# A hard-max attention kernel: four query tiles loaded between the first key halves, first transposes copied in half columns by two engines, a group's key chosen in five steps

## The chip, the cores and the metric

The kernel runs on one core of a Trainium2 chip. The metric is device microseconds for one execution, as the median of several. The profile is a separate reading of one such execution: its span, from the first to the last instruction, is 1.7 to 1.9 us less than the time that is measured for the same execution, so spans are compared with spans and medians with medians.

Engines in the profile: PE is TensorE, DVE is VectorE, ACT is ScalarE, POOL is GpSimd, SP is SyncE.

## The reference

```
q, k, v: (4, 4096, 128) float32, normal random numbers
logits = q @ k.transpose            # per batch, 4096 x 4096
out[b, i] = v[b, argmax(logits[b, i])]
```

It is attention whose softmax is replaced by the single best key. Every output row must be the right row of `v`, so near ties have to be found and settled exactly.

## The kernel before

A query tile is 128 queries, and there are 128 tiles in all, 32 to a batch. The 4096 keys of a batch are taken in 1024 groups of four. TensorE multiplies the queries with sums and differences of the keys of a pair, and the larger of the two logits of a pair is the sum part plus the absolute difference part. Per tile this takes three evictions of 128x1024 on ScalarE (two `A`, one `E`) and one on VectorE (`W`, the *fold*, which takes the maximum of the two pairs). `W` carries a score in the upper half of each word and the group's number in the lower half. `MAX8` then gives the best groups of each query.

```
def dpart(t, x):                                  # differences of pair x: |d|
    ps = pp.tile([P, 1024], FP32, tag="u")
    mm(ps, t, 1 + 2 * x, True)
    nc.scalar.activation(out=A, in_=ps, func=AF.Abs)

def spart(t, x):                                  # sums of pair x, plus A
    ...
    if x == 0:
        nc.scalar.activation(out=E, in_=ps, func=AF.Relu, scale=QSCALE)

def fold(t):                                      # VectorE: max of the two pairs
    nc.vector.scalar_tensor_tensor(out=W_t[t % NW].bitcast(I16)[:, 1::2], in0=ps, scalar=QSCALE, in1=E,
                                   op0=OP.mult, op1=OP.max)
def top(t):
    nc.vector.max(out=TOP[:, t, :], in_=W_t[t % NW].bitcast(FP32))
```

For every tile GpSimd then gathers the best group's three key differences (`kg`, fp16). VectorE multiplies them with the queries (`prod`), folds the products twice (`p`) and sums them (`D`). For 8 tiles at a time (4 near the end) it chooses the best of the four keys, and GpSimd gathers that key's row of `v` (`vr`):

```
near = (d + NEAR) >= mx                           # which of the four are near the best
CNT  = sum(near)                                  # over 1: the row is flagged
lt   = d < mx
sel  = lt * 2**20 + iotab[b]
wi   = min(sel)                                   # number of the best, first one of equals
win  = cand * 4 + wi
for j in range(n):
    nc.gpsimd.indirect_dma_start(out=vr[:, j, :], in_=v_flat, in_offset=IOA(ap=win[:, j:j + 1], axis=0))
```

(shortened to formulas; with the maximum `mx` in front these are seven VectorE instructions.) Flagged rows are computed again exactly, in two segments. The second comes at the very end: GpSimd fetches the record `FR`, the query `FQ`, three key groups `FK` and the value `FV` of each flagged row and writes them to the output.

The start-up is what the change mostly rearranges:

```
for h in range(2):
    load_k(0, h, 0, 16)                           # key halves, fp32 -> fp16, GpSimd's queue
load_q(0, 0, 8)                                   # 8 query tiles behind them
load_q(0, 8, NQT)
... warm-up matmuls, identity ...
for h in range(2):
    put_k(0, h)                                   # kd: key differences for the gathers
...
def trn_half(b, u, h):                            # transposes of key unit u, half h
    ...
    if h == 1:
        nc.scalar.activation(out=kT[...1024 columns...], in_=ps, func=AF.Copy)
...
for u in (1, 3, 0, 2):
    trn_half(0, u, 0)
trn_half(0, 1, 1)
trn_q(0, 0)                                       # 8 query tiles, one copy by ScalarE
trn_half(0, 3, 1)
trn_half(0, 0, 1)
dpart(0, 0)
trn_half(0, 2, 1)
dpart(0, 1)
```

## Time and profile before

| | before |
|---|---|
| median | 471.05 us (4 runs, 470.95 to 471.29) |
| span of the profiled run | 469.4 us |
| first fold starts | 19.82 us |
| last fold starts | 416.07 us |
| first gather of the end's flags (`FR`) | 433.66 us |
| final write of the flagged rows | 458.48 us |

The view by windows gives the busy time of each engine in a stretch. Its columns are the stretch, its length, then busy us of TensorE, its weight loads, VectorE, ScalarE and GpSimd, with the number of instructions in brackets, the granted clock, the DMA share and GB/s. Of the kernel before:

```profile
core 0: us, PE busy (x) PEld busy (x) DVE busy (x) ACT busy (x) POOL busy (x), PEclk, DMA share, GB/s
...
60.00:150.00 90.00, 85.08 (x418) 38.18 (x417) 90.00 (x163) 86.68 (x105) 58.57 (x65) 1.00 0.51 99
150.00:300.00 150.00, 138.02 (x674) 61.51 (x673) 149.21 (x288) 139.67 (x166) 108.10 (x119) 1.00 0.60 116
300.00:400.00 100.00, 89.97 (x389) 37.32 (x388) 100.00 (x207) 91.12 (x99) 70.36 (x72) 1.00 0.31 85
```

VectorE is busy 339.2 of 340 us: it sets the pace of the long middle. ScalarE (317.5 us) and TensorE (313.1 us) are not far behind.

The timeline lists instructions by start, with duration and, in brackets, the engine's idle time just before and what ended it. VectorE's start-up, before:

```profile
4.24 1.29 DVE L100 CAST identh<-ident 128x128 f16<-128x128 f32 x1 [3.11 <-POOL ident masks.py:199]
...
19.82 1.31 DVE L224 SCALAR_TENSOR_TENSOR W<-psn,E 128x1024 int16<-128x1024 f32 x1 [8.42 <-ACT E L211]
```

TensorE's, before. The three lines show when the two key halves and the queries have landed (for the first half the wait stands with TensorE's weight load, 0.61 us until 6.52):

```profile
6.53 0.23 PE L151 MATMUL tk<-identh,natk 128*128 128x128 f16 x1
...
8.98 0.23 PE L151 MATMUL tk<-identh,natk 128*128 128x128 f16 x1 [0.49 <-DMA natk<-in_k_dram]
...
11.28 1.04 PE L178 MATMUL tq<-identh,natq 128*128 128x128 f16 x8 [1.67 <-DMA natq<-in_q_dram]
```

ScalarE's, before: the first distance eviction and the first `E`, with a key copy between the evictions (left out).

```profile
15.08 1.04 ACT L198 ACTIVATE A<-pd 128x1024 f16<-128x1024 f32 x1
...
18.69 1.09 ACT L211 ACTIVATE E<-psn 128x1024 int16<-128x1024 f32 x1
```

So VectorE waits for ScalarE, ScalarE for TensorE, and TensorE for the queries, which come last.

The tail belongs to GpSimd. Its timeline near the end, before:

```profile
393.50 0.94 POOL L246 DMA_INDIRECT kg<-k,cand  x1 [0.66 <-DVE near L283]
...
431.16 0.94 POOL L303 DMA_INDIRECT vr<-in_v_dram,win  x1 [0.30 <-issue]
432.41 0.94 POOL L303 DMA_INDIRECT vr<-in_v_dram,win  x1 [0.30 <-issue]
433.66 1.09 POOL L495 DMA_INDIRECT FR<-rec,rr_e  x1 [0.30 <-DVE row_e L492]
```

From 393.50 us to `FR` at 433.66 GpSimd starts 32 gathers and scatters every 1.25 us without another wait: 40.16 us.

### The profile page before, as it was taken

The numbers are of one execution on the slowest core, as the hardware profiler recorded it, in microseconds if no ns is written. First come the engines' busy times: TensorE is split into PE (matmuls) and PEld (weight loads), VectorE is DVE, ScalarE is ACT, GpSimd is POOL, SyncE is SP. The second block draws the span as 40 slices with busy tenths as digits, with TensorE's granted clock in tenths as the row PEclk, the third lists the DMA queues.
The fourth block names the chain that finished last, engine by engine and source line by source line (L and its number), as shares of the span: only waits on it lengthen the run. The fifth ranks groups of instructions, "written<-read, shape, count | busy, mean of one in ns | idle before, by whom it ended". The sixth has DMA issues, their size and how long they took to land. (4 is left out here: it accounts for less than half of the span.)

```text
span 469.4 us, 6266 instructions
## 1 busy us (share of the span) xinstructions
PE 381.8 (81%) x1840; PEld 169.8 (36%) x1840; DVE 417.2 (89%) x845; ACT 379.7 (81%) x438; POOL 305.8 (65%) x345
## 2 busy tenths in 40 slices
PE   7999999999999889999998889999999889920000
PEld 3544444444444334444443434343333333300000
DVE  4189999999999999999999999999999999998400
ACT  1999999999999899999998889999999879910000
POOL 9124445876667887766677876667777567777740
PEclk9899999999999999999999999999999999975555
DMA  7913489462224969642336864232433132324320
GB/s 135 231 31 81 79 129 124 91 137 69 86 74 99 193 110 161 117 113 59 101 92 146 119 123 94 69 98 64 120 90 110 51 100 57 113 66 122 104 79 5
DMA packets 40776, 47.42 MB, mean 101 GB/s; under 512 B 24200, under 2 KB 32395, under 8 KB 40736
## 3 DMA queue, kind: packets, MB, share of 16 engines
q0 software_dynamic: 18464, 30.97, 33.9%
q1 hardware_dynamic: 22272, 16.00, 13.2%
q8 instruction: 15, 0.25, 0.2%
q14 instruction: 25, 0.20, 0.2%
HBM read 39.59 MB, written 12.19 MB: 110 GB/s over the span
## 5 line engine op out<-in xcount | busy, mean ns | idle before, releaser
L198 ACT ACTIVATE A<-pd 128x1024 f16<-128x1024 f32 x256 | 258.8, 1042 | 17.2 <-PE pd L189 17.0
L246 POOL DMA_INDIRECT kg<-k,cand x128 | 126.2, 986 | 100.5 <-DVE p L265 25.2
L224 DVE SCALAR_TENSOR_TENSOR W<-psn,E 128x1024 int16<-128x1024 f32 x128 | 167.6, 1309 | 13.1 <-ACT E L211 11.9
L189 PE MATMUL pd<-kT,qT 128*128 128x512 f16 x512 | 152.3, 379 | 15.1 <-ACT A L198 14.4
L189 PE MATMUL psn<-kT,qT 128*128 128x512 f16 x512 | 151.8, 378 | 14.0 <-ACT A L198 9.0
L228 DVE MAX8 TOP<-W 128x8 f32<-128x1024 f32 x128 | 157.5, 1231 | 0.0
L189 PEld LDWEIGHTS <-qT 128*128 128x128 f16 x1024 | 98.5, 97 | 162.0 <-issue 74.7
L208 PE MATMUL psn<-A,identh 128*128 128x512 f16 x512 | 152.1, 378 | 0.0
L303 POOL DMA_INDIRECT vr<-in_v_dram,win x128 | 126.5, 988 | 39.0 <-issue 37.2
L211 ACT ACTIVATE E<-psn 128x1024 int16<-128x1024 f32 x128 | 132.3, 1034 | 5.5 <-PE psn L208 5.1
L208 PEld LDWEIGHTS <-identh 128*128 128x128 f16 x512 | 49.6, 97 | 60.8
L261 DVE TENSOR_TENSOR prod<-kg,natq 128x768 f16<-128x768 f16 x64 | 35.7, 559 | 1.1 <-DMA kg<-k,cand 1.1
L265 DVE TENSOR_TENSOR p<-prod 128x384 f16<-128x384 f16 x64 | 22.9, 361 | 0.0
L270 DVE TENSOR_REDUCE D<-p 128x6 f32<-128x192 f16 x64 | 22.2, 349 | 0.0
L167 ACT ACTIVATE kT<-uk 128x256 f16<-128x256 f32 x48 | 20.1, 418 | 0.9 <-PE uk L164 0.9
L268 DVE TENSOR_TENSOR p<-p 128x192 f16<-128x192 f16 x64 | 16.4, 259 | 0.0
L163 PE MATMUL uk<-identh,natk 128*128 128x128 f16 x96 | 15.8, 218 | 0.5 <-ACT A L198 0.5
L63 POOL DMA_DIRECT2D natk<-in_k_dram x26 | 15.6, 603 | 0.9 <-POOLq L778 0.8
L66 POOL DMA_DIRECT2D natq<-in_q_dram x26 | 15.7, 607 | 0.0
L461 PE MATMUL fp_e<-n_e,tri 128*128 128x1 f32 x2 | 0.6, 361 | 16.2 <-DVE n_e L459 16.2
L164 PEld LDWEIGHTS <-natk 128*128 128x128 f16 x96 | 9.3, 97 | 7.6 <-issue 5.1
L163 PEld LDWEIGHTS <-natk 128*128 128x128 f16 x96 | 9.3, 97 | 5.6
(148 smaller groups left out, 146.8 us busy)
## 6 DMA issues: line engine op xcount, KB each, us to landing
out_dram<-vr SPq DMA_DIRECT2D x14, 512.0 KB, 2.9
k<-kd SPq DMA_DIRECT2D x8, 384.0 KB, 2.6
natk<-in_k_dram POOLq DMA_DIRECT2D x24, 128.0 KB, 3.7
natq<-in_q_dram POOLq DMA_DIRECT2D x24, 128.0 KB, 3.1
kg<-k,cand POOLq DMA_INDIRECT x128, 2.7
vr<-in_v_dram,win POOLq DMA_INDIRECT x128, 3.3
natk<-in_k_dram POOLq DMA_DIRECT2D x2, 512.0 KB, 7.0
out_dram<-vr SPq DMA_DIRECT2D x4, 256.0 KB, 2.1
```

The costliest lines, as they stand in the source:

```text
L163: nc.tensor.matmul(out=o, lhsT=natk[b % 2][:, h, 4 * m + x, :], rhs=identh, start=True, stop=False)
L189: nc.tensor.matmul(out=ps[:, n * 512:(n + 1) * 512], lhsT=qT[b % 2][:, qt * P:(qt + 1) * P], rhs=kT[b % 2][:, u * 1024 + n * 512:u * 1024 ...
L198: nc.scalar.activation(out=A, in_=ps, func=AF.Abs)
L208: nc.tensor.matmul(out=ps[:, n * 512:(n + 1) * 512], lhsT=identh, rhs=A[:, n * 512:(n + 1) * 512], start=False, stop=True)
L211: nc.scalar.activation(out=E, in_=ps, func=AF.Relu, scale=QSCALE)
L224: nc.vector.scalar_tensor_tensor(out=W_t[t % NW].bitcast(I16)[:, 1::2], in0=ps, scalar=QSCALE, in1=E, op0=OP.mult, op1=OP.max)
L228: nc.vector.max(out=TOP[:, t, :], in_=W_t[t % NW].bitcast(FP32))
L246: near_q.append(lambda j=j: nc.gpsimd.indirect_dma_start(out=kg[:, j].rearrange("p f d -> p (f d)"), out_offset=None, in_=k16[t0 // NQT], ...
L261: nc.vector.tensor_tensor(out=prod, in0=kg, in1=natq[b % 2][:, x - b * NQT:x - b * NQT + m, :].unsqueeze(2).to_broadcast([P, m, 3, P]), op ...
L265: nc.vector.tensor_tensor(out=p1, in0=prod[:, :, :, 0:64], in1=prod[:, :, :, 64:128], op=OP.add)
L270: nc.vector.tensor_reduce(out=d[:, x - c0:x - c0 + m, 1:4], in_=p2, axis=AX_X, op=OP.add)
L303: late_q.append(lambda j=j: nc.gpsimd.indirect_dma_start(out=vr[:, j, :], out_offset=None, in_=v_flat, in_offset=IOA(ap=win[:, j:j + 1], a ...
```

## The change

There are two intentions. In the start-up, four query tiles (not eight) are to land between the key halves, and VectorE is to share the copies of the transposed keys, so that the first distance can be evicted earlier. In the choosing, `lt`, the old `sel` and `min` go, and one product of `near` with the keys' numbers comes in, so that seven instructions become five. Each of the four keys gets a number from 8 to 11, and the sum of the numbers of all near keys tells both which key it is (8 to 11) and whether there were several (17 or more, hence the new threshold of 12). Where several are near, the sum points to a wrong row, perhaps one beyond the end of `v`, so the gather gets a bounds check; such rows are flagged and computed again. Group numbers are now counted in keys (multiples of four), which saves the multiplication. Cut to its core:

```
-    for h in range(2):
-        load_k(0, h, 0, 16)
-    load_q(0, 0, 8)
-    load_q(0, 8, NQT)
+    load_k(0, 0, 0, 16)
+    load_q(0, 0, 4)
 ... warm-up (7 instead of 8 matmuls twice), identity ...
+    load_k(0, 1, 0, 8)
+    load_k(0, 1, 8, 16)
+    load_q(0, 4, 8)
+    load_q(0, 8, NQT)
 ...
-    for h in range(2):
-        put_k(0, h)
 ...
+    ALL = range(4)
+    trn_half(1, 0, ALL, by_act)
+    trn_half(3, 0, ALL, by_dve)
+    trn_half(0, 0, ALL, by_act)
+    trn_q(0, 4, by_dve)
+    trn_half(2, 0, ALL, by_act)
+    put_k(0, 0)
     for u in (1, 3, 0, 2):
-        trn_half(0, u, 0)
-    trn_half(0, 1, 1)
-    trn_q(0, 0)
-    trn_half(0, 3, 1)
-    trn_half(0, 0, 1)
+        trn_half(u, 1, (0, 1))
+    trn_half(1, 1, (2, 3), by_act)
+    trn_half(3, 1, (2, 3), by_dve)
+    trn_half(0, 1, (2, 3), by_dve)
+    trn_half(2, 1, (2, 3), by_dve)
     dpart(0, 0)
-    trn_half(0, 2, 1)
     dpart(0, 1)
 ... put_k(0, 1) and the next four query tiles (by DMA transpose) go behind the first fold ...

         near = (d + NEAR) >= mx
-        CNT = sum(near);  lt = d < mx;  sel = lt * 2**20 + iotab[b];  wi = min(sel)     # as formulas
-        nc.vector.scalar_tensor_tensor(out=win, in0=cand, scalar=4.0, in1=wi, op0=OP.mult, op1=OP.add)
+        nc.vector.tensor_tensor(out=sel, in0=near, in1=iota8.unsqueeze(1).to_broadcast([P, n, 4]), op=OP.mult)
+        nc.vector.tensor_reduce(out=CNT[:, t0:t1], in_=sel, axis=AX_X, op=OP.add)
+        nc.vector.scalar_tensor_tensor(out=win, in0=CNT[:, t0:t1], scalar=float(b * Sk - 8), in1=cand, op0=OP.add, op1=OP.add)
 ...
             late_q.append(lambda j=j: nc.gpsimd.indirect_dma_start(out=vr[:, j, :], ...,
-                                                                   in_offset=IOA(ap=win[:, j:j + 1], axis=0)))
+                                                                   in_offset=IOA(ap=win[:, j:j + 1], axis=0),
+                                                                   bounds_check=B * Sk - 1, oob_is_err=False))
```

## The prediction

> **What bounds the kernel now.** The windows view shows VectorE busy 90.0 of 90 us from 60 to 150 us, 149.2 of 150 from 150 to 300 and 100 of 100 from 300 to 400; ScalarE is at 96, 93 and 91%. So from about 45 us to 415 us VectorE paces. Before that there are two phases. Start-up: VectorE's first fold begins at 19.82 us (timeline), after 8.42 us of waiting for ScalarE. Then, to about 34 us, ScalarE paces: tiles follow at 2.75 us (three 128x1024 evictions) and VectorE has small gaps (1.44, 0.34, 0.34, 0.27, 0.93). After the last fold there is a tail of 50 us in which GpSimd issues gathers back to back (0.94 us plus 0.30 between) from 393.5 to 436 us, and again after 446.
>
> **Start-up, costed.** Before: key halves land at 6.5 and 8.96 us, the query piece only at 11.27 (timeline of PE); then ScalarE does query, two key copies, and the first distance eviction starts at 15.08; with one more key copy in between, E of tile 0 starts at 18.69. After: 256 KB of queries go between the halves, so the second half lands later by about 0.6 us (1 MB took 2.46 us), at about 9.6. ScalarE copies only four 128x512 pieces (about 0.5 us), VectorE five (about 0.6, half of the 1.2 us pitch of a 128x1024 fold). [...] First distance eviction at about 11.2, E of tile 0 at about 13.9, first fold at about 15.0: 4.8 us earlier. The second key difference (0.97 us) moves behind the first fold, into the 1.44 us gap: free. Query tiles 4-8 by DMA transpose have some 5 us to spare.
>
> **Steady phase.** Two of seven choosing steps go. Each shows 0.19 us but takes only 0.09 us start to start between independent instructions. 14 groups before the tail: 14 x 2 x 0.09 = 2.5 us, all on VectorE, hence critical.
>
> **Added on GpSimd.** The 128 value gathers get a bounds check. In the quiet tail bounded gathers take 1.00 us, unbounded 0.94: 0.06 x 128 = 7.7 us. GpSimd has about 45 us of waits for VectorE between 40 and 393, so most is hidden. In the tail it shows: 17 of the 32 gathers between the last such wait (393.5) and the first flag gather are value gathers: +1.0 us. The choosing chain gets one dependent step before the count (+0.2 us, hidden behind GpSimd). In return one value gather fewer stands behind the last flag gather: -1.1 us. Tail: about 0.
>
> **Sum.** -4.8 - 2.5 - 0.1 = -7.4: 463.8 us, range 460.5 to 467.5. Chances: faster by over 2% 0.20, within 2% 0.79, slower 0.01.
>
> **What would show it.** First fold at 14 to 16.5 us; five VectorE copies of about 0.6 us; fold 100 about 6.5 us earlier; 36 fewer choosing instructions; value gathers at about 1.00 us at best; VectorE still 99% busy from 60 to 400; the flag gather in the tail about 6 us earlier, the end about 7.
>
> **What would make it wrong.** Key or query pieces landing later than 10 us (start-up gain under 3 us); VectorE copies blocked by GpSimd's iotas (over 1.2 us each); bounded gathers slowing GpSimd so that VectorE's products wait for gathered keys, or a larger GpSimd backlog at 393, which would return part of the steady gain in the tail; ScalarE, freed of nothing in the steady phase, becoming the pacer.

(A sentence with a reason for its figure of about 0.6 us, which no trace of this case shows, is cut. No term of the sum is cut with it: it came to -4.8 - 2.5 - 0.1 = -7.4 us, 463.8 us, as it stands. The risk of copies "blocked by GpSimd's iotas (over 1.2 us each)" rests on the two 128x128 conversions of the kernel before, which took 1.29 and 1.21 us beside them. The 5 us to spare for the transposed queries are the author's estimate; in the changed kernel the first two transposes are issued from 11.45 us and through by 17.99, and the fold of tile 4 comes at 27.37.)

## More of the kernel before

The view of waits sums idle time by what ended it (total, number, longest). VectorE between 20 and 410 us, before:

```profile
DVE W L224 <- ACT E L211: 11.9, 7, 8.4
DVE W L224 <- PE psn L208: 1.2, 3, 0.6
DVE prod L261 <- DMA kg<-k,cand: 0.2, 1, 0.2
```

## The result, and the profile after

The changed kernel takes 467.5 us (4 runs, 467.32 to 468.39) against 471.05 us. The ratio is 0.9928, with a 95% interval of 0.9911 to 0.9945. Ratios here and below are the mean time of one kernel's fast runs over that of the other's fast runs of the same rounds, so they are not quite the ratios of the medians. A later repetition on another chip gave 467.35 against 471.27 us, ratio 0.9924. So the change gains 3.6 to 3.9 us where 7.3 were predicted, and the median lies on the upper end of the range.

Windows, after:

```profile
60.00:150.00 90.00, 85.21 (x417) 38.04 (x415) 90.00 (x157) 86.87 (x105) 66.41 (x69) 1.00 0.49 104
150.00:300.00 150.00, 137.60 (x677) 61.65 (x676) 148.70 (x277) 139.51 (x166) 112.88 (x117) 1.00 0.57 116
300.00:400.00 100.00, 90.55 (x390) 37.54 (x389) 99.79 (x198) 91.93 (x99) 72.72 (x72) 1.00 0.30 85
```

VectorE still sets the pace (338.5 of 340 us). VectorE's start-up, after:

```profile
3.18 0.23 DVE L103 CAST identh<-ident 128x128 f16<-128x128 f32 x1 [2.04 <-POOL ident masks.py:199]
3.32 0.22 DVE L105 TENSOR_SCALAR identn<-ident 128x128 f16<-128x128 f32 x1
...
7.62 0.69 DVE L161 CAST kT<-tk 128x512 f16<-128x512 f32 x1 [3.96 <-PE tk L152]
8.29 0.69 DVE L161 CAST qT<-tq 128x512 f16<-128x512 f32 x1
...
11.51 1.89 DVE L161 CAST kT<-tk 128x512 f16<-128x512 f32 x3 [1.67 <-PE tk L152]
...
16.37 1.31 DVE L228 SCALAR_TENSOR_TENSOR W<-psn,E 128x1024 int16<-128x1024 f32 x1 [2.84 <-ACT E L215]
```

The first fold comes 3.45 us earlier, and the five copies take 0.68 or 0.69 us each. TensorE's, after: queries by 7.86 (no wait in front of them), the two pieces of the second key half at 9.54 and 10.85 us, the first distance at 11.94.

```profile
7.86 0.39 PE L182 MATMUL tq<-identh,natq 128*128 128x128 f16 x4
...
9.54 0.23 PE L151 MATMUL tk<-identh,natk 128*128 128x128 f16 x1 [0.57 <-DMA natk<-in_k_dram]
...
10.85 0.23 PE L151 MATMUL tk<-identh,natk 128*128 128x128 f16 x1 [0.25 <-DMA natk<-in_k_dram]
...
11.94 1.29 PE L193 MATMUL pd<-kT,qT 128*128 128x512 f16 x5
```

ScalarE's, after:

```profile
12.56 2.85 ACT L202 ACTIVATE A<-pd 128x1024 f16<-128x1024 f32 x3 [0.68 <-PE pd L193]
15.29 1.04 ACT L215 ACTIVATE E<-psn 128x1024 int16<-128x1024 f32 x1
```

GpSimd in the tail, after:

```profile
388.46 0.96 POOL L250 DMA_INDIRECT kg<-k,cand  x1 [1.07 <-DVE near L287]
...
398.79 1.25 POOL L300 DMA_INDIRECT vr<-in_v_dram,win  x1 [0.30 <-issue]
400.34 1.01 POOL L300 DMA_INDIRECT vr<-in_v_dram,win  x1 [0.31 <-issue]
...
427.61 1.39 POOL L300 DMA_INDIRECT vr<-in_v_dram,win  x1 [0.30 <-issue]
429.30 1.00 POOL L300 DMA_INDIRECT vr<-in_v_dram,win  x1 [0.30 <-DVE rw_e L485]
430.60 1.00 POOL L493 DMA_INDIRECT FR<-rec,rr_e  x1 [0.30 <-DVE n_e L505]
```

The same 32 gathers, from 388.46 to `FR` at 430.60, now take 42.14 us instead of 40.16. The usual value gather takes 1.00 us instead of 0.94, and a few take 1.25 or 1.39.

VectorE's waits between 20 and 410 us, after:

```profile
DVE W L228 <- ACT E L215: 2.6, 6, 0.9
DVE W L228 <- PE psn L212: 1.1, 3, 0.6
DVE prod L265 <- DMA kg<-k,cand: 0.8, 1, 0.8
```

The first line before held the 8.42 us in front of the first fold, which after lies ahead of this stretch. The third has grown from 0.2: near 180 us VectorE stands still for 0.78 us because gathered keys are late (1.05 us in the later repetition).

Laid end to end, by the two timelines (us; the sum is that of the spans, 469.40 to 465.55, and to 466.14 in the repetition):

| stretch | predicted | measured | repeated |
|---|---|---|---|
| start to first fold | -4.8 | -3.45 | -3.15 |
| first fold to last fold | -2.5 | -1.92 | -1.52 |
| last fold to GpSimd's last wait | none given | +0.33 | +0.31 |
| that wait to `FR` (32 gathers) | +1.0 | +1.98 | +2.00 |
| `FR` to the final write | -1.1 | -0.97 | -1.08 |
| final write to the end | none given | +0.18 | +0.18 |
| sum | -7.4 | -3.85 | -3.26 |

("Repeated" is the profile of the later repetition against the same profile of before; that one profiled run was among the slower ones of its kernel, 467.91 us, and its span was 466.1. A first fold is known to half a microsecond: two later kernels with the old start-up have theirs at 19.34 and 19.36 us instead of 19.82; their eight query transposes on TensorE take 0.62 us, those of the kernel before 1.04.)

Three terms are short of what was forecast: the start by 1.3 to 1.6 us (or more, with the 19.35), the middle with what follows it by 0.9 to 1.3, the 32 gathers by 1.0.

### The profile page after: what moved, and what is told of

Its sections match the earlier page's. It is cut to its first block, busy times and chain, and to the rows that moved or that the text cites. A ratio compares the mean times of both kernels' runs of the same rounds, so it can differ in the third digit from the quotient of the medians.

```text
span 465.6 us, 6352 instructions
## 1 busy us (share of the span) xinstructions
PE 379.1 (81%) x1834; PEld 168.3 (36%) x1834; DVE 414.5 (89%) x814; ACT 376.8 (81%) x437; POOL 319.7 (69%) x345
## 5 line engine op out<-in xcount | busy, mean ns | idle before, releaser
L228 DVE SCALAR_TENSOR_TENSOR W<-psn,E 128x1024 int16<-128x1024 f32 x128 | 169.8, 1326 | 6.8 <-ACT E L215 5.5
L300 POOL DMA_INDIRECT vr<-in_v_dram,win x128 | 138.5, 1082 | 39.0 <-issue 37.8
L232 DVE MAX8 TOP<-W 128x8 f32<-128x1024 f32 x128 | 159.7, 1248 | 0.0
L265 DVE TENSOR_TENSOR prod<-kg,natq 128x768 f16<-128x768 f16 x64 | 36.8, 577 | 3.7 <-DMA kg<-k,cand 3.7
L269 DVE TENSOR_TENSOR p<-prod 128x384 f16<-128x384 f16 x64 | 24.1, 379 | 0.0
L274 DVE TENSOR_REDUCE D<-p 128x6 f32<-128x192 f16 x64 | 23.2, 366 | 0.0
L272 DVE TENSOR_TENSOR p<-p 128x192 f16<-128x192 f16 x64 | 17.5, 276 | 0.0
L170 PEld LDWEIGHTS <-natk 128*128 128x128 f16 x96 | 9.3, 97 | 7.7 <-issue 5.3
L244 DVE TENSOR_SCALAR cand<-TOP 128x2 uint32<-128x2 uint32 x64 | 11.9, 187 | 0.0
```

The costliest lines, as they stand in the source:

```text
L265: nc.vector.tensor_tensor(out=prod, in0=kg, in1=natq[b % 2][:, x - b * NQT:x - b * NQT + m, :].unsqueeze(2).to_broadcast([P, m, 3, P]), op ...
L269: nc.vector.tensor_tensor(out=p1, in0=prod[:, :, :, 0:64], in1=prod[:, :, :, 64:128], op=OP.add)
L274: nc.vector.tensor_reduce(out=d[:, x - c0:x - c0 + m, 1:4], in_=p2, axis=AX_X, op=OP.add)
L300: late_q.append(lambda j=j: nc.gpsimd.indirect_dma_start(out=vr[:, j, :], out_offset=None, in_=v_flat, in_offset=IOA(ap=win[:, j:j + 1], a ...
```

## The experiments

All kernels gave correct results. They were made in five groups on several chips. In three groups the kernel before took 471 us. On one chip, which came up for two groups, it took 509 us at a lowered granted clock (0.92 to 0.94 over the whole span of the kernels there, 0.94 elsewhere; in windows in the middle it falls to 0.93 to 0.97 instead of 1.00). Times of that chip are compared with nothing but its own runs of the kernel before. Medians are over all runs, ratios over the fast ones; one run of the kernel before there (549.22 us at a clock of 0.72) was the slowest of those left out of the ratios.

### The two halves of the change by themselves

The kernel before with the start-up part alone (loads, transposes, copies, as in the diff above):

> The start-up part of the change alone (loads, transposes, copies on two engines, later key difference); seven choosing steps and unchecked gathers as before. If the start-up shift is carried rigidly to the end, first fold at 16.4 us, last fold about 412.6, and the whole 3.4 us faster than before (about 467.6). If a backlog on GpSimd swallows a start-up gain in the tail, the last fold is 3.4 us earlier but the end only 1.5 to 2.5 us.

Measured: 468.30 us against 471.26, ratio 0.9939 (0.9923 to 0.9956). First fold at 16.55 us, last fold at 412.61, as a rigid shift would have it, `FR` at 430.74. The tail gives back 0.57 us: its 32 gathers, the same instructions as before, take 40.73 us instead of 40.16.

The kernel before with the choosing part alone (group numbers, five steps, bounds check):

> The choosing part alone (key index in units of rows, five steps, bounds check on the value gathers), start-up as before. First fold at 19.8 as before; last fold about 1.9 us earlier than before; but the end within 0.5 us of before (about 470.8), since the tail gives back about 1.6 us. If the two parts interact and choosing is worth its steps on its own, the end is 1.5 to 2.5 us earlier.

Measured: 470.48 us against 471.26, ratio 0.998 (0.9966 to 0.9995). From first to last fold it takes 394.24 us instead of 396.25, so the steps save 2.0 us there, against 1.52 to 1.92 in the whole change. But the 32 gathers take 42.53 instead of 40.16 us, and after `FR` it gains 0.9 us. Of a gain of 2.9 us in two stretches, 2.4 are paid back in the stretch between them.

The two parts add: 2.96 + 0.78 = 3.74 us, and the whole gains 3.6 to 3.9.

### The bounds check

The changed kernel without the check (right for this draw of the inputs only, as no row points outside), and the kernel before with the check:

```
-                                            in_offset=IOA(ap=win[:, j:j + 1], axis=0),
-                                            bounds_check=B * Sk - 1, oob_is_err=False))
+                                            in_offset=IOA(ap=win[:, j:j + 1], axis=0)))
```

> The changed kernel without the bounds check on the value gathers (for this draw no chosen row is out of range, worked out beforehand). Theory check: value gathers go from a median of 1.01 back to 0.94 us, the stall of VectorE on a key gather near 180 us (0.78 us) goes, and the end is 1.2 to 2.4 us earlier than the changed kernel (about 465.1 to 466.3). Rival order: the loss in the tail comes from the changed order of gathers on GpSimd, the check is hidden, and the time is within 0.4 us of the changed kernel.

> The kernel before with nothing but the bounds check added to its value gathers. Theory check: value gathers at about 1.01 us, the last fold within 0.6 us of before, the tail longer, the end 1.2 to 2.4 us later than before (472.3 to 473.5). Rival order: within 0.4 us of before.

Measured: without the check 466.12 us against 471.26 (0.9887, 0.9871 to 0.9902), 1.4 us less than the changed kernel on another chip (1.2 to 1.6 less if each one's gain over its own kernel before is compared); with the check alone 472.98 (1.0035, 1.0021 to 1.0049), 1.7 us more than before. The median value gather is 0.94 us without and 1.01 with. In the kernel with the check alone, first to last fold takes 396.34 us as before (396.25), and the 32 gathers take 42.06 us instead of 40.16: the cost lies where GpSimd has no gap. One thing expected did not come: the stall near 180 us stays without the check (0.75 us), so the check is not its cause. It comes with the five steps: eight of the nine full-clock profiles with five steps have it (0.46 to 1.20 us, between 179.6 and 185.8 us; the last kernel below does not), and none of the three with seven.

### The order of instructions

The new choosing has two steps fewer, so that everything behind it moves. In this kernel two empty turns in the schedule put it back:

```
         yield "dve",
+        yield "dve",
+        yield "dve",
         win = ...
```

> The changed kernel with two empty steps put where the two choosing steps were taken out, so that the program order of gathers on GpSimd and of the flag work is that of before. Theory order: VectorE's stall on a key gather near 180 us (0.75 to 0.8 us in all kernels with the five steps, with or without the check) and the 0.3 us near 276 us go, the last fold comes about 0.7 us earlier relative to the first fold (a gain after the first fold of about 2.6 instead of 1.95 us); but one more value gather stands behind the last flag gather, 1.3 us, so the end is 0 to 0.8 us later than the changed kernel. Rival: the stall is DMA weather, or comes of VectorE being early; then it stays, and the end is 1.0 to 1.6 us later.

Measured: 468.67 us against 471.36, ratio 0.9944 (0.9931 to 0.9958), 1.2 us slower than the changed kernel. The stretch of 32 gathers is the same (42.17), a stall stays (0.46 us at 185.8), and the difference is after `FR`, where one value gather more stands behind `FV` (12.84 us from `FV` to the final write instead of 11.62). So the order explains the 1.1 us that were predicted there, and it does not explain the loss in the tail, nor more than a part of the stall.

### Three rivals for the start-up

The second key half in one piece; the query piece behind both key halves; all loads issued ahead of the identity:

```
 (1)  -    load_k(0, 1, 0, 8)          (2)  -    load_q(0, 0, 4)   (ahead of the second half)
      -    load_k(0, 1, 8, 16)              +    load_q(0, 0, 4)   (behind it; trn_q last, by ScalarE)
      +    load_k(0, 1, 0, 16)         (3)  the four later loads moved ahead of make_identity
```

> The changed kernel with the second key half loaded in one piece. Theory small query piece (the 256 KB of queries move at half the rate and delay all behind them): the half lands at about 10.8 us as the second quarter does now, and as no part of it can be transposed before, the first fold is 0.4 to 1.0 us later (17.0 to 17.6). Rival split (smaller pieces move slower): the half lands by 10.2 us and the first fold is not later than 16.8.

> The changed kernel with the query piece loaded behind the key halves, not between them, and transposed last (copied by ScalarE). Theory small query piece: key quarters land at about 7.9 and 9.2 us, the query piece at about 10.4; first distance eviction near 12.0 instead of 12.6, first fold 0.3 to 0.8 us earlier, the end likewise (about 0.1 per cent). Rival (the time to the last landing is set by bytes and issue alone, any order): the query piece lands at 10.8 us or later and the first fold is not earlier.

> The changed kernel with all its first loads issued before the identity is built on GpSimd, as before. Rival issue (the 0.6 us of identity work between the issues starves the DMA engines): second quarter lands at about 10.2 us, first fold about 0.6 us earlier. Theory small query piece: landing and first fold unchanged within 0.25 us, which is the scatter of the first fold between equal programs so far (16.37, 16.55, 16.82).

| | second half landed | first fold | median us | ratio |
|---|---|---|---|---|
| changed kernel | 10.85 | 16.37 (repeated 16.67) | 467.5 | 0.9928 |
| (1) one piece | 10.58 | 16.99 | 467.79 | 0.9921 |
| (2) queries third | 10.04 | 16.64 | 467.84 | 0.9937 |
| (3) loads first | 11.10 | 16.62 | 467.85 | 0.9926 |

None is faster. The first folds of kernels with the same start-up scatter by 0.45 us (16.37 to 16.82), so their differences here mean little. The landings of the last piece scatter too, from 10.85 to 11.30 in the five full-clock profiles with the changed kernel's start-up, and the changed kernel's own is the earliest of them; (2) lies clear of that. Putting the queries behind takes 0.8 us off the landing, but then the queries come last. Issuing earlier, in (3), leaves the landing where it was; besides, VectorE's cast of the identity there meets GpSimd's index patterns and takes 1.28 us instead of 0.23.

### Three remedies, on the chip with the lowered clock

First, the eight loads of a batch's two-ahead keys spread over every other tile instead of eight in a row. Second, the four keys numbered 11, 10, 9, 8 and the sum subtracted, so that only the first batch's gathers can leave `v` (at its start) and only they keep the check. Third, the four query tiles on SyncE's queue in fp32, cast by VectorE, with the second key half right behind the first. Fourth, all three.

```
-    elif 18 <= qt < 26:                      +    if qt >= 17 and qt % 2:
-        load_part(b + 2, qt - 18)            +        load_part(b + 2, (qt - 17) // 2)

-    win = CNT + (b * Sk - 8) + cand          +    win = cand + (b * Sk + 11) - CNT     # iota8 = 11, 10, 9, 8
-    bounds_check=B * Sk - 1, ...             +    the same, for b == 0 only

-    load_q(0, 0, 4)                          +    load_k(0, 1, 0, 16)
                                              +    nc.sync.dma_start(out=q4, in_=...q tiles 0 to 3...)
                                              +    nc.vector.tensor_copy(out=natq[0][:, 0:4], in_=q4)
```

> The changed kernel with the eight key loads of the batch after next spread over every second tile (17 to 31 of a batch) where they now follow each other tile by tile (18 to 25). Theory cadence: from about 160 to 190 us GpSimd issues a key gather, a value gather and a load per tile, 3.20 us, gapless, so a VectorE with less to do runs into it: then the stall on a key gather (0.8 to 1.2 us) goes, the last fold comes 0.6 to 1.0 us earlier after the first fold (2.5 to 2.9 instead of 1.95), and the end 0.4 to 1.0 us earlier. Rival (VectorE is capped there by the 3.06 us of a tile on ScalarE and TensorE, not by GpSimd): the waits turn into waits for TensorE and the last fold gains less than 0.3 us.

> The changed kernel with the choosing weights reversed (11, 10, 9, 8, subtracted), so that a row with several near keys can only point too low: the bounds check is then needed in the first batch alone and goes from the other 96 value gathers, those of the tail among them. Theory check: value gathers of the tail at 0.94 us, the end like the kernel without any check, 1.0 to 1.8 us earlier than the changed kernel (about 466.1). Rival order: within 0.4 us of the changed kernel.

> The changed kernel with the first four query tiles loaded in fp32 from the queue of SyncE and cast by VectorE, and the second key half in one piece right behind the first on GpSimd's queue. Theory pieces (what was late is not bytes: small pieces between the key halves on GpSimd's queue run at a fraction of the rate): the second half lands at 9.0 to 9.6 us, first fold at 14.6 to 15.6, the end 1.0 to 1.8 us earlier than the changed kernel. Rival bytes (the landing is set by the bytes on the 16 DMA engines): the second half lands at 10.3 us or later, first fold at 16.0 or later.

> The three together: query piece from SyncE, check in the first batch alone, spread key loads. If the effects add, the end is 2.4 to 4.2 us earlier than the changed kernel: 463.3 to 465.1. If the tail on GpSimd caps it (gathers there are back to back), what the start and the middle gain before it still arrives, as the tail starts from VectorE's last key candidates; a gain under 2 us would speak against that.

Then again. The third differs: ScalarE casts the queries. The chip was the same one.

> The changed kernel, with the eight loads of a batch's two-ahead queries and keys spread over every other tile of the second half of the batch instead of eight tiles in a row. Theory (GpSimd's cadence): the changed kernel's faster chooser ran into GpSimd, which had no gap between 160 and 190 us; spread, the stall of VectorE near 180 us (0.78 us) goes, the last fold ends 0.6 to 1.0 us earlier than in the changed kernel (410.70 us) and the end is 0.4 to 1.0 us earlier. Rival (the tile cap on ScalarE and TensorE takes the gain as well): the last fold moves by less than 0.3 us, the end likewise.

> The changed kernel, with the order of the four keys counted down from 11 so that the window's start can never be negative beyond the first batch, and the bounds check on the first batch's gathers only. Theory (the check costs GpSimd time in the tail, where it is the limit): median value gather 0.94 us instead of 1.01, the end 1.0 to 1.8 us earlier than the changed kernel's 467.5, about 466.1, as without any check. Rival (the gain of the kernel without a check came from something else than the check): the end within 0.4 us of the changed kernel.

> The changed kernel, with the first four query tiles loaded uncast on SyncE's queue and cast by ScalarE, and the second key half in one piece right behind the first on GpSimd's queue. Theory (the query piece and the small pieces on GpSimd's queue delay the second half): the second half lands at 9.0 to 9.8 us instead of 10.85, the first fold ends at 14.6 to 15.6 us instead of 16.37, the end is 1.0 to 1.8 us earlier. Rival (the bytes as such set the landing, on whichever queue): the second half lands at 10.3 us or later, the first fold within 0.4 us of the changed kernel.

> The three edits together: spread loads, reversed order with the check on the first batch alone, queries on SyncE's queue with ScalarE's cast. If the three causes are separate and each holds, the gains add: 2.4 to 4.2 us earlier than the changed kernel, 463.3 to 465.1 us. If one of them falls, the sum is less by its part; if they share a limit, the sum is less than the three single ones.

| | first time, before 509.0 us | ratio | second time, before 509.5 us | ratio |
|---|---|---|---|---|
| spread loads | 490.61 | 0.968 (0.9615 to 0.9745) | 492.44 | 0.9679 (0.9625 to 0.9734) |
| reversed numbers | 504.16 | 0.9933 (0.9874 to 0.9991) | 505.47 | 0.9919 (0.9866 to 0.9973) |
| queries by SyncE | 508.15 | 1.0035 (0.9971 to 1.0099) | 505.80 | 0.991 (0.9848 to 0.9973) |
| all three | 495.73 | 0.9721 (0.9638 to 0.9804) | 496.14 | 0.9743 (0.9688 to 0.9798) |

At this clock VectorE waits at changing places, mostly for TensorE (the longest wait is 6.0 us), so the expected differences of 1 us can't be read from these times. Three things can. The spread loads are 2.3 to 3.5% faster than the kernels that have the rest of the change, twice over; why they profit so much there was not tested, and the changed kernel itself never ran on this chip. All three remedies together are no faster than the spread loads alone, so nothing adds up here as it was expected to. The median value gather with the reversed numbers is 0.95 us. And the start-up, where VectorE's first cast (0.23 us) and first fold (1.31 us) take what they take at full clock, shows why queries by SyncE did not help. VectorE, third remedy with ScalarE's cast:

```profile
3.18 0.23 DVE L103 CAST identh<-ident 128x128 f16<-128x128 f32 x1 [2.05 <-POOL ident masks.py:199]
3.32 4.99 DVE L105 TENSOR_SCALAR identn<-ident 128x128 f16<-128x128 f32 x1
6.36 1.96 DVE L161 CAST qT<-tq 128x512 f16<-128x512 f32 x1
...
16.31 1.31 DVE L228 SCALAR_TENSOR_TENSOR W<-psn,E 128x1024 int16<-128x1024 f32 x1 [3.41 <-ACT E L215]
```

TensorE never waits for the second key half here. But the negative identity takes 4.99 us where the changed kernel took 0.22, until GpSimd's three long index patterns (4.19 to 7.89 us) are through, and the query copy behind it ends only at 8.3 us. With VectorE's cast (first time) the same befell that cast: 4.84 us. The limit only moved. Why the negative identity was held up here and not in the changed kernel, where it starts at the same 3.32 us beside a load that GpSimd issues, is not shown.

### All remedies, and the cast taken off VectorE, at full clock

```
-    nc.vector.tensor_scalar(out=identn, in0=ident, scalar1=-1.0, ...)
+    nc.scalar.activation(out=identn, in_=ident, func=AF.Copy, scale=-1.0)
-    trn_q(0, 4, by_dve)
+    trn_q(0, 4, by_act)
     trn_half(0, 1, ALL, by_dve)
+    dpart(0, 0)
     trn_half(2, 1, ALL, by_dve)
-    dpart(0, 0)
```

(on top of the three remedies), and the changed kernel itself once more, on the same chip:

> The three edits of the former kernel, and three more in the start-up, since there the second key half landed by 9.4 us and the first fold still ended its wait at 16.3: the negative identity is made by ScalarE (on VectorE it took 4.98 us beside GpSimd's iotas), the query copy goes to ScalarE, and the first distance is put ahead of the last key unit on TensorE. Theory (VectorE's cast beside the iotas took the place of the landing as the limit): the first distance eviction starts at 11.0 to 11.7 us instead of 12.5, the first fold at 14.8 to 15.7 us. Rival (ScalarE's chain of three evictions and the copies sets it): the first fold within 0.4 us of 16.3. On a chip with a full clock the whole is 2.4 to 4.5 us earlier than the changed kernel's 467.5: 463.0 to 465.1 us; of it the stretch from the first fold to the last 0.6 to 1.0, the tail 1.0 to 1.8. On the chip with the lowered clock: earlier than the changed kernel of the same call by about 12 us, since the spread loads did that against the kernel before.

> The changed kernel itself, so that it stands beside the other on the same chip whatever its clock. On a chip with a full clock 467.5 us within 0.5, ratio to the kernel before 0.993. On the chip with the lowered clock about 505 us, ratio 0.99: what the kernels there gain beyond that ratio is then theirs and not the change's.

Measured: 465.88 us for the first, 467.35 for the second, against 471.27 us; ratios 0.9898 (0.9883 to 0.9913) and 0.9924 (0.9909 to 0.9939). All remedies together are 1.5 us faster than the changed kernel, the best of all valid ones, but 0.8 us short of the least that was expected. Its start-up, VectorE:

```profile
10.98 2.02 DVE L162 CAST kT<-tk 128x512 f16<-128x512 f32 x3 [0.96 <-PE tk L153]
...
15.66 1.31 DVE L229 SCALAR_TENSOR_TENSOR W<-psn,E 128x1024 int16<-128x1024 f32 x1 [2.44 <-ACT E L216]
```

and TensorE, which now waits for the landing again:

```profile
9.88 0.23 PE L152 MATMUL tk<-identh,natk 128*128 128x128 f16 x1 [0.55 <-DMA natk<-in_k_dram]
```

The first fold is at 15.66 us, 0.7 to 1.0 earlier than in the changed kernel and inside what was expected. The first distance eviction starts at 11.86, just outside what was expected (11.0 to 11.7).

The middle gains only 0.13 us over the one profile of the changed kernel and 0.53 over the other (394.20 us from first to last fold, against 394.33 and 394.73), where 0.6 to 1.0 were expected. Its waits show why:

```profile
DVE W L229 <- ACT E L216: 2.0, 5, 0.9
DVE W L229 <- PE psn L213: 1.9, 6, 0.6
```

No wait for gathered keys is left, as expected. In its place the folds wait for TensorE more often (1.9 us in 6 waits, against 1.1 in 3), at 170.9, 174.4 and 180.8 us, where the stall had been. So here the rival is mostly right: an engine that is spared one wait meets the next one. As this kernel has six edits, what each is worth is not shown. The 32 gathers take 41.64 us, 0.5 less than with the check on all batches, against 40.16 before the change; 1.0 to 1.8 had been expected for the tail.

### What the long gathers are

Without any check the 32 gathers still take 41.44 us in the changed order, 1.28 more than before, though the usual gather is at 0.94 us again. The rest is a few long ones. VectorE at the two long ones of the changed kernel's tail shown above:

```profile
398.61 0.55 DVE L265 TENSOR_TENSOR prod<-kg,natq 128x768 f16<-128x768 f16 x1
399.07 1.22 DVE L232 MAX8 TOP<-W 128x8 f32<-128x1024 f32 x1
...
426.84 1.29 DVE L470 TENSOR_TENSOR OH_e<-iota_h,posn_e 128x512 bf16<-128x512 f16 x2
428.05 0.21 DVE L475 TENSOR_REDUCE n_e<-F_e 128x1 f32<-128x64 f32 x1
```

The gather of 398.79 us starts inside a product of two SBUF tensors, which ends at 399.07, when VectorE's next instruction starts: 0.28 us remain, and the gather takes 1.25, 0.25 more than usual. The gather of 427.61 starts 0.44 us before the end of another one and takes 0.39 more.

This was counted from 60 us on in the traces of nine kernels at full clock (before, changed, its repetition, and the six that change one part or all). Take the gathers that start at least 0.03 us after a `prod`, with at least 0.08 us of it left. All 80 are longer than their median by what is left, within 0.07 us, 0.16 to 0.24 us each on average. (Of eight more that start with the product, within 0.03 us, three keep their usual length.) The folding of the products, `p`, has two SBUF inputs as well, and 87 of the 88 gathers that start inside it are longer by what is left. The contrast is with instructions that have one SBUF input: of 1249 gathers that start in the same way inside the fold `W`, `MAX8` or the sum `D`, one is over 0.1 us longer. And of 190 gathers that start 0.03 to 0.3 us *ahead* of a `prod`, 8 are. Nor is the product held up then: the 24 products of the kernel before that start 0.03 to 0.3 us after a gather, while that runs on for 0.94 us or more, take their usual 0.53 to 0.60 us. That it is the two SBUF inputs is the author's reading: `prod` and `p` also share an operation (TENSOR_TENSOR) that the other three do not have, and no run separates the two. It is a strong order in time, found by looking and not by an experiment that moves the products. The start-up part alone comes nearest to one: its tail has the instructions of before, only earlier, and there a gather of 427.70 us starts with the product of two SBUF tensors that the one of 427.61 above met, and takes 0.54 us more. It says that the number of long gathers in the tail depends on where such instructions fall between them. In the changed kernel four gathers of the tail are long, all inside such an instruction (398.79, 414.52, 415.94 and 427.61 us), together by 0.87 us; before, one is, by 0.08.

## Why the prediction was right or wrong

**What bounds the kernel: right.** VectorE sets the pace from 60 to 400 us before and after, ScalarE's evictions of one tile (2.75 us) set it at the start, up to about 34 us before and 31 after, GpSimd in the tail.

**Choosing: the steps right, "hence critical" only in part.** The prediction had 36 fewer instructions, and there are: 14 groups in front of the tail, each giving 2 x 0.09 us, "all on VectorE, hence critical". The work did go: between first and last fold VectorE is busy 391.4 us before and 388.6 with the choosing alone, 392.2 with the start-up alone and 389.6 with both, so 2.6 to 2.8 us less, 0.19 to 0.20 for each group. (The start-up part adds 0.8 us there, as the second key difference moves behind the first fold; its waits for ScalarE shrink by as much, so that is free, as forecast.) But the kernel with this part alone gains 2.0 us in the middle, the changed kernel 1.5 to 1.9. The rest comes back as waits, most of it 0.71 to 1.05 us for gathered keys near 180 us. In the last kernel that wait is gone and waits for TensorE have grown, which suggests, without showing it, that the middle is close to a common limit of three engines (from 160 to 190 us of that kernel VectorE is busy 29.08, ScalarE 28.22 and TensorE 27.61 of 30 us). The prediction had named the stall ("VectorE's products wait for gathered keys"), but among the risks, without a size in the sum, and gave bounded gathers as its cause, which the run without the check does not bear out.

**Start-up: the mechanism right, the landing mis-sized.** This is the first step that failed: "256 KB of queries go between the halves, so the second half lands later by about 0.6 us ... at about 9.6". The last piece landed at 10.85, so 1.9 us later than in the kernel before and not 0.6 (up to 11.30 in the other profiles with this start-up). All that follows then came as reckoned: from the first distance eviction to the first fold the prediction had 3.8 us (11.2 to 15.0), and it took 3.81 (12.56 to 16.37). The landings of the experiments divide the delay. The second half lands at 8.98 us with no queries ahead of it, at 9.88 with the queries at the same time on another queue, at 10.58 with the queries ahead on the same queue, at 10.85 in two pieces besides. So some 0.9 us go with the bytes, and the remaining 1.0 with the place in the queue and the pieces. These two can't be told apart by adding: two pieces alone, with no queries ahead of them (trial 2), land at 10.04, 1.1 us late, the queries alone (trial 1) make it 1.6, both together 1.9. The kernels differ in other loads too, so these are estimates from single landings, with a scatter of up to 0.45 us.

The data rate over the first 12 us, in 40 slices of 0.3 us, before:

```profile
GB/s 0 0 0 0 0 0 0 0 41 68 14 96 205 218 218 218 205 218 218 191 219 218 205 205 191 205 205 150 191 177 109 96 109 96 96 253 184 184 246 164
```

and after, where it sinks from 218 to between 51 and 130 from 6.6 to 8.1 us (the 23rd to 27th slice):

```profile
GB/s 0 0 0 0 0 0 0 0 27 191 0 27 177 218 218 218 205 218 205 123 184 167 51 109 109 102 130 150 171 191 219 218 198 184 225 236 283 205 205 246
```

(The profile counts bytes as they land, in fp16, a key half as 512 KB; the 256 KB of the prediction are fp32, as they are read.) What moves slowly there is not the query piece but the load behind it. The queries come in packets of 1 KB, and these are through by 6.8 us, at 123 to 184 GB/s. The view of DMA for 7.0 to 8.0 us counts 53 packets, all of the key piece:

```profile
DMA packets 53, 0.11 MB, mean 109 GB/s; under 512 B 0, under 2 KB 0, under 8 KB 53
```

From 9.0 to 9.6 us the same pieces move at 218 GB/s. So, by these rates, the queries' own transfer cost about 0.7 us, near the 0.6 of the forecast, and what the forecast lacked is about 1.0 us for the slow first stretch of the load behind them. (Both are estimates from the line above.) Trial (2), with that load straight behind the first half and no queries ahead, is as slow from 6.0 to 8.0 us (125 GB/s), and the last kernel, which issues the whole second half at once behind the first, is not (207 GB/s). So the queries' bytes are not what slows it; what does is not shown. The lines of before held a warning: the queries there, 512 KB of fp32 behind the keys, took 2.3 us from 8.98 to 11.28, so half of them 1.15. Read from those, the landing would have been forecast at 10.1, still 0.7 short, and the first fold at 15.5.

**VectorE's copies: right.** Forecast about 0.6 us each, with "blocked by GpSimd's iotas (over 1.2 us each)" among the risks. Measured 0.68 to 0.69, and not blocked: the two at 7.62 and 8.29 us took 0.69 each beside GpSimd's index patterns (5.22 to 8.96 us). So these copies from PSUM kept their time. The casts from SBUF to SBUF are the opposite: 0.22 and 0.23 us in the changed kernel with no index pattern beside them, 1.29 (before), 1.28 (trial 3) and 4.99 us beside GpSimd's index patterns. The cast of the kernel before (4.24 to 5.53 us) ends 0.08 us after the first index pattern (4.17 to 5.45). The 4.99 us are longer than any one instruction of GpSimd there and last through three of its index patterns, of 1.3 us each. What holds the casts up, and not the copies, is not shown.

**The tail: right in sign, half the size.** The second step that failed is "17 of the 32 gathers ... are value gathers: +1.0 us". There are 19, and 19 x 0.06 = 1.1 us is what the check costs there. Another 0.9 us come from long gathers, a term which the sum did not have. The stretch lengthened by 1.98. Three trials bear on it: the check alone adds 1.9 us to the 32 gathers of the kernel before (1.1 and some long ones), the check taken off saves 0.7 of the changed kernel's, and the last kernel, with reversed numbers and the check on one batch, saves 0.5. In the last two the usual value gather is back at 1.25 us from start to start (1.31 with the check), so 1.1 us are saved, and more long gathers take a part of it away. The -1.1 us for one value gather fewer behind the last flag gather came as forecast (-0.97 to -1.08), and the run with the old order confirms its cause.

**What would show it.** Fold 100 comes 4.95 us earlier (forecast 6.5), `FR` 3.06 (forecast 6), the end 3.8 (forecast 7). The first fold at 16.37 was inside the forecast band of 14 to 16.5, but at its edge, and repeated at 16.67, outside it. The list of what could go wrong named landings "later than 10 us" with a gain under 3 us; the landing came true, and the gain was 3.15 to 3.45 in the two profiles (2.7 to 3.0 against a first fold of 19.35).

**Open.** Whether the products' place in time is what makes the long gathers was not tested by moving them. The stall near 180 us is absent from the last kernel, which spreads the loads but changes other things too; on the chip with the lowered clock all four kernels with spread loads still have one there, of 0.64 to 1.99 us (the two with reversed numbers and loads in a row 0.42 and 0.48). So its cause is not shown, and those runs speak against the loads in a row. Why a load behind the first half starts slowly, and why spread loads gain so much at a lowered clock, is unknown. And the 0.31 to 0.33 us between the last fold and GpSimd's last wait, and the 0.18 us between the final write and the end, are not explained.

## What to carry to other kernels

Split a predicted gain by stage and ask in each stage which engine sets the pace: 2 us saved on VectorE here were nearly all paid back in the tail, where GpSimd works without a gap and a check of 0.06 us per gather counts in full. Take a load's cost from the same kind of load in the same place of the queue in the trace, not from the best rate next to it (here 0.6 us from the keys' rate, 1.15 from the queries before, 1.6 measured in trial 1). And when a wait is removed, look for the second one behind it before counting the gain: the landing gave way to a blocked cast, the late keys to a late TensorE.
